# A second buffer for one decay tile, and two steps of the scan placed behind the projection in a Mamba-2 layer

## The chip, the cores and the metric

The kernel runs on one core of one Trainium2 chip. The metric is device time in microseconds, as the median of several runs. The engines are PE (TensorE: matmuls, with PEld for its weight loads), DVE (VectorE), ACT (ScalarE), POOL (GpSimd) and SP (SyncE), whose queue issues the DMAs. Each engine takes its instructions in the order of its own queue.

## The reference

Two layers run over a context pass of 128 tokens and a denoising pass of 512 tokens, with shared weights and width 1024. Layer 0 is gated attention; the change doesn't touch it. Layer 1 is a bidirectional Mamba-2 scan in chunks of 128 tokens, so there are five tiles of tokens: tile 0 is the context, tiles 1 to 4 are the denoising pass. What matters here, for each of four groups of eight heads:

```
proj = h @ w_in;  z, xbc, dt = split(proj)
xbc  = silu(depthwise_conv(xbc, width 3))          # x, B and C
cb     = C @ B^T                                    # per tile, 128 x 128
y_diag = (cb * decay) @ x                           # decay: exp of differences of cumulative sums, per head
states = B^T @ (x * decay_end)
h      = h * chunk_decay + states                   # from tile to tile
y_off  = (C @ h_prev) * exp(a_cs)
y = y_forward + flip(y_backward) + d_skip * x
out = rms_norm(y * silu(z)) @ w_out
```

Both directions have a decay tile of their own. The kernel adds the two before it multiplies by C.B, so one diagonal product per tile serves both.

## The kernel before, in words

Matrix products of activations and weights are done as three products of high and low parts. `split` makes a high part (a cast on ScalarE, L73) and a low part (a difference on VectorE or GpSimd, L74). Weights come through `raw` tiles (two buffers) and become `wh` and `wl` tiles.

Layer 1 works through four groups `g` of heads. In each there are ten steps `j`. Steps 1 to 5 deal with one tile each in the order `seq = [0, 2, 3, 1, 4]`. In a step the source lists, in this order:

- `mix` (L1127, L1128): the product C.B of the tile of the step before on PE, into a slot of the PSUM pool `a` (four slots), then the decay tile `am0` is multiplied by it on VectorE.
- `off` (L1173 to L1175) and `advance` (L1179, L1182, L1183) for both directions: the product of C and the state, scaled and added to `Y`, and the new state.
- `decay` (L1116, L1117, L1121, L1122): two affine selects on GpSimd, sixteen exponentials on ScalarE, and GpSimd's sum of the two directions' tiles `am0` and `am1`.
- `diag` (L1135, L1138 to L1140): sixteen products of the decay tile with x into a PSUM slot, four transposes of `Y` into another, a copy on ScalarE and a sum on VectorE. After `diag` the `am0` buffer is free.
- `a_load` (L1112): the loads of the next tile's `am0` (two buffers) and `am1` (one buffer), 512 KB each, on SP's queue.
- the fill: the projection of a chunk of the next group's x, B or C (`proj_T`, L914: 48 matmuls into one of two `pj` tiles of PSUM), its convolution on VectorE (L994 to L996, tanh L998 on ScalarE, L999), the transposes of the chunk before (L1007), or a chunk of z (L1057, L1058). In the last group the fill holds z, the turn of finished tiles (L1354, L1357) and the first matmuls of the output weights (L1368).

`gate` and `gate_last` (L1086, L1094 to L1098) multiply `Y` by the gate and add up its squares. `final_rstd` (L1373, L1374) sums the squares over partitions.

The kernel is built with `schedule_with_timeline_sim=True`: a planner plays the program through with costs of its own and sets the order on each engine from that. The order in the source is a priority, and no more; an instruction that isn't ready in the planner's account is overtaken. `high_priority(offset=300)` moves the priority of what it encloses ahead by 300; `issue_after(i)` puts what it encloses, on the engine of instruction `i`, behind `i`.

## Time and profile before

| what | value |
|---|---|
| runs | 994.69, 998.58 and 999.16 us, median 998.58 |
| profiled execution | 996.55 us, of which the span is 994.8 |
| PE busy | 937.9 us, 94% |
| DVE, ACT, POOL busy | 656.3 (66%), 515.3 (52%), 431.1 us (43%) |
| mean granted clock of PE over the span | 0.981 of full speed |

Busy time is the time in which an engine has an instruction in work. Matmuls overlap, so a matmul's own duration is longer than its distance to the next. The granted clock is 1.00 (2.4 GHz) or 0.50 (1.2 GHz) at any moment. In a row of the order in time, the bracket at the end is the time that the engine stood idle before it, and what it waited for. "A <- B: 7.5, 2, 5.2" in a list of waits says that A waited for B 7.5 us in total, twice, and 5.2 us at the longest.

### The profile page before, as it was taken

The page shows a single profiled execution, that of the slowest core. Times are in us where ns is not written, and L with a number is a line of the kernel's source. Part 1 is how long each engine was busy: PE and PEld are TensorE (multiplying, and loading weights), DVE is VectorE, ACT ScalarE, POOL GpSimd, SP SyncE. Part 2 cuts the span into 40 slices and gives each one's busy share as a digit, 9 for nine tenths or more (in the row PEclk, how much of TensorE's full clock was granted, in tenths as well). Part 3 has the DMA queues.
Part 4 walks back from the last instruction along what each step waited for, and adds up shares of the span by engine and source line. Part 5 has one row for each costly group of instructions (what it writes and reads, how often), then busy time and mean ns, then how long its engine had stood idle before and what let it go on. Part 6 is the DMA issues. An engine that isn't in the chain of part 4 may idle for free. (4 is left out here: it accounts for less than half of the span.)

```text
span 994.8 us, 17000 instructions
## 1 busy us (share of the span) xinstructions
PE 937.9 (94%) x6466; PEld 835.0 (84%) x6466; DVE 656.3 (66%) x1046; ACT 515.3 (52%) x1212; POOL 431.1 (43%) x415
## 2 busy tenths in 40 slices
PE   5998999999999989989899979999999999989998
PEld 3897879879997789989898878889988898658786
DVE  5468665666675764884759854956587547797663
ACT  5355666757775763433446564446436642554240
POOL 3345235227270162364267475739484853333000
PEclk9999999999999989999999999999999999989999
DMA  9942234221113222333234352344524441455752
GB/s 319 351 128 87 86 127 138 67 73 43 37 49 107 85 93 100 123 106 89 86 131 148 121 181 88 109 139 145 151 87 146 156 133 64 128 183 190 257 194 96
DMA packets 90354, 127.91 MB, mean 129 GB/s; under 512 B 6816, under 2 KB 65312, under 8 KB 90272
## 3 DMA queue, kind: packets, MB, share of 16 engines
q1 hardware_dynamic: 90272, 126.82, 39.6%
q8 instruction: 51, 0.84, 0.3%
q14 instruction: 31, 0.25, 0.1%
HBM read 115.10 MB, written 11.70 MB: 127 GB/s over the span
## 5 line engine op out<-in xcount | busy, mean ns | idle before, releaser
L914 PE MATMUL pj<-h,wh 128*128 128x322 f32 (+1 forms) x1248 | 298.3, 325 | 8.7 <-DVE B L999 7.5
L914 PEld LDWEIGHTS pj<-h,wh 128*128 128x128 f32 (+1 forms) x1248 | 211.2, 189 | 21.5 <-issue 14.0
L74 POOL TENSOR_TENSOR wl<-raw,wh 128x512 fp32r<-128x512 f32 (+1 forms) x70 | 133.1, 1912 | 184.6 <-ACT wh L73 182.9
L914 PE MATMUL pj<-h,wl 128*128 128x322 f32 (+1 forms) x624 | 198.6, 319 | 0.0
L73 ACT CAST wh<-raw 128x1024 fp32r<-128x1024 f32 (+1 forms) x117 | 103.0, 912 | 79.7 <-DMA raw<-in_l_w_out 22.4
L1121 ACT ACTIVATE am<-am,nb 128x128 f32<-128x128 f32 x320 | 97.9, 389 | 62.4 <-POOL am L1117 39.9
L914 PEld LDWEIGHTS pj<-h,wl 128*128 128x128 f32 (+1 forms) x624 | 118.2, 190 | 3.9 <-issue 3.6
L283 PE MATMUL pp<-wh,big 128*128 128x256 f32 x576 | 112.1, 284 | 0.5 <-ACT sg L527 0.5
L283 PEld LDWEIGHTS pp<-wh,big 128*128 128x128 f32 x576 | 91.2, 188 | 0.9 <-ACT sg L527 0.7
L74 DVE TENSOR_TENSOR wl<-raw,wh 128x1024 fp32r<-128x1024 f32 x47 | 62.8, 1347 | 38.0 <-ACT wh L73 38.0
L283 PE MATMUL pp<-wl,big 128*128 128x256 f32 x288 | 81.1, 282 | 0.0
L74 DVE TENSOR_TENSOR pl<-pt,ph 128x512 fp32r<-128x512 f32 (+1 forms) x100 | 59.2, 599 | 25.9 <-ACT ph L73 25.1
L633 DVE TENSOR_REDUCE nm<-S 128x1 f32<-128x640 f32 x64 | 52.3, 819 | 13.7 <-PE S L630 12.7
L73 ACT CAST ph<-pt 128x512 fp32r<-128x512 f32 (+1 forms) x100 | 51.4, 517 | 19.1 <-PE pt L658 14.3
L1122 POOL TENSOR_TENSOR am<-am,am 128x1024 f32<-128x1024 f32 x20 | 48.7, 2437 | 26.2 <-ACT am L1121 26.2
L637 ACT ACTIVATE Pt<-S,nm 128x640 f32<-128x640 f32 x64 | 51.2, 802 | 13.4 <-PE pt L658 9.9
L1368 PE MATMUL pj<-wh,h 128*128 128x512 f32 x160 | 54.4, 413 | 0.5 <-ACT wh L73 0.5
L283 PEld LDWEIGHTS pp<-wl,big 128*128 128x128 f32 x288 | 54.3, 188 | 0.0
L658 PE MATMUL pt<-cst,Pt 128*128 128x128 f32 x320 | 51.6, 279 | 2.6 <-DVE pl L74 2.3
L630 PE MATMUL S<-kT,qT 128*128 128x320 f32 x256 | 51.1, 324 | 2.3 <-ACT Pt L637 2.3
L1116 POOL TENSOR_SCALAR_AFFINE_SELECT am<-am 128x1024 f32<-128x1024 f32 x20 | 24.2, 1211 | 56.6 <-DMA am<-acd 32.3
L658 PEld LDWEIGHTS pt<-cst,Pt 128*128 128x128 f32 x320 | 37.2, 142 | 11.8 <-PE S L630 3.7
(347 smaller groups left out, 2135.9 us busy)
## 6 DMA issues: line engine op xcount, KB each, us to landing
raw<-in_l_w_in SPq DMA_DIRECT2D x48, 512.0 KB
am<-acd SPq DMA_DIRECT2D x40, 512.0 KB
raw<-in_l_w_out SPq DMA_DIRECT2D x36, 512.0 KB
og<-in_l_mod_w SPq DMA_DIRECT2D x29, 512.0 KB
raw<-in_l_w_in SPq DMA_DIRECT2D x25, 256.0 KB
mw<-in_l_mod_w SPq DMA_DIRECT2D x11, 512.0 KB
raw<-in_l_mod_w SPq DMA_DIRECT2D x8, 512.0 KB
yzd<-ys SPq DMA_DIRECT2D x6, 640.0 KB
```

The costliest lines, as they stand in the source:

```text
L73: (heng.tensor_copy if heng else self.nc.scalar.copy)(hi, src)
L74: (eng or self.nc.vector).tensor_tensor(lo, src, r32(hi), op=ALU.subtract)
L283: nc.tensor.matmul(ps, a[:, k, cs], b[:, k, :], start=k == 0 and a is hi and b is w[0], stop=k == KD - 1 and a is lo)
L630: nc.tensor.matmul(S[:, 192 + 320 * q:512 + 320 * q], qTs[g, t][:, h, :], kT[:, hl, 320 * q:320 * q + 320], start=hl == 0, stop=hl == 1)
L633: nc.vector.tensor_reduce(c["m"], c["s"], axis=AX.X, op=ALU.max, negate=True)
L637: nc.scalar.activation(Pt, c["s"], AF.Exp, bias=c["m"], scale=1.0, accum_out=rss[g][t][:, h:h + 1])
L658: nc.tensor.transpose(pt[:, 2 * i + j, :], Pts[j][:, kt * P:kt * P + P], self.ident)
L914: nc.tensor.matmul(ps[0:m, 190 + 322 * half:512 + 322 * half], w[b][:, k, off:off + m], hT[s][:, k, 322 * half:322 * half + 322], start=fi ...
L1116: nc.gpsimd.affine_select(out=af[0], in_=af[0], pattern=[[0, 8], [1, P]], base=0, channel_multiplier=-1, compare_op=ALU.is_ge, fill=NEG)
L1121: nc.scalar.activation(af[d][:, h, :], af[d][:, h, :], AF.Exp, bias=self.nb[:, t, i:i + 1], scale=1.0)
L1122: nc.gpsimd.tensor_tensor(af[0], af[0], af[1], op=ALU.add)
L1368: nc.tensor.matmul(self.PS[t][n], y[a][:, kk, :], b, start=k0 + k == 0 and i == 0, stop=k0 + k == 15 and i == 2)
```

## The change

The second direction's decay tile `am1` gets two buffers (in every place that uses the tag). The five instructions of a convolution get a priority ahead by 300. `mix` and `diag` move behind the fill of their step, and `mix` on VectorE is tied behind the last VectorE instruction that was listed before it. In the last group `final_rstd` comes two steps later than `gate_last`.

```
--- before.py
+++ after.py
@@ -68,6 +68,9 @@
         kw = {} if space is None else {"space": space}
         p = self.tc.tile_pool(name=name, bufs=bufs, side=side, reuse_waits="tile", **kw) if space != DRAM else self.tc.tile_pool(name=name, bufs=bufs, space=DRAM)
         return ctx.enter_context(p)
+
+    def last_on(self, engine):
+        return next(i for i in reversed(self.nc.cur_bb.bb.instructions) if i.engine == engine)
 
     def split(self, hi, lo, src, eng=None, heng=None):
         (heng.tensor_copy if heng else self.nc.scalar.copy)(hi, src)
@@ -922,7 +925,7 @@
         nc.sync.dma_start(out=misc[:, 200:], in_=A["cst"][:, 3 * P + 2:])
         upper, lower = misc[:, 200:200 + P], misc[:, 200 + P:]
         ones, al, db = misc[:, 0:P], misc[:, P:P + 64], misc[0:64, 199:200]
-        packs = [self.tl(wk, [P, 3, NT, 64], tag=t_, bufs=b_) for t_, b_ in (("am0", 2), ("am0", 2), ("am1", 1))]
+        packs = [self.tl(wk, [P, 3, NT, 64], tag=t_, bufs=b_) for t_, b_ in (("am0", 2), ("am0", 2), ("am1", 2))]
         slots = iter([p_[:, i] for p_ in packs for i in range(3)])
         self.dsk = self.tl(sp, [P, SH], tag="dsk")
         for d, s in enumerate(("f", "b")):
@@ -991,12 +994,13 @@
         ps = self.proj_T(pj, w, off, P, hT)
         cb0 = self.col["l1_conv_b"][0]
         n = TW - 3
-        nc.vector.tensor_scalar(out=u, in0=ps[:, 1:1 + n], scalar1=self.cw[:, 24 + j:25 + j], scalar2=self.cols[:, cb0 + j:cb0 + j + 1], op0=ALU.mult, op1=ALU.add)
-        nc.vector.scalar_tensor_tensor(out=u, in0=ps[:, 0:n], scalar=self.cw[:, j:j + 1], in1=u, op0=ALU.mult, op1=ALU.add)
-        nc.vector.scalar_tensor_tensor(out=u, in0=ps[:, 2:2 + n], scalar=self.cw[:, 48 + j:49 + j], in1=u, op0=ALU.mult, op1=ALU.add)
         th = ps[:, 1:1 + n]
-        nc.scalar.activation(th, u, AF.Tanh)
-        nc.vector.scalar_tensor_tensor(out=u, in0=th, scalar=1.0, in1=u, op0=ALU.add, op1=ALU.mult)
+        with self.tc.high_priority(offset=300):
+            nc.vector.tensor_scalar(out=u, in0=th, scalar1=self.cw[:, 24 + j:25 + j], scalar2=self.cols[:, cb0 + j:cb0 + j + 1], op0=ALU.mult, op1=ALU.add)
+            nc.vector.scalar_tensor_tensor(out=u, in0=ps[:, 0:n], scalar=self.cw[:, j:j + 1], in1=u, op0=ALU.mult, op1=ALU.add)
+            nc.vector.scalar_tensor_tensor(out=u, in0=ps[:, 2:2 + n], scalar=self.cw[:, 48 + j:49 + j], in1=u, op0=ALU.mult, op1=ALU.add)
+            nc.scalar.activation(th, u, AF.Tanh)
+            nc.vector.scalar_tensor_tensor(out=u, in0=th, scalar=1.0, in1=u, op0=ALU.add, op1=ALU.mult)
         return u
 
     def turn(self, u, pa, put):
@@ -1107,7 +1111,7 @@
             nc.gpsimd.tensor_tensor(h3(y), h3(xts[g][:, t, :]), bch(self.dsk[:, 8 * g:8 * g + 8]), op=ALU.mult)
 
         def a_load(g, t):
-            af = W[g, t] = [self.tl(wk, [P, 8, P], tag=f"am{d}", bufs=2 - d) for d in range(2)]
+            af = W[g, t] = [self.tl(wk, [P, 8, P], tag=f"am{d}", bufs=2) for d in range(2)]
             for d in range(2):
                 nc.sync.dma_start(out=af[d].rearrange("p h l -> p (h l)"), in_=self.acd[t][g][d].rearrange("h l -> (h l)").unsqueeze(0).to_broadcast([P, 8 * P]))
 
@@ -1238,8 +1242,6 @@
                 fl = {j: [nx(j)] for j in range(4)}
                 fl.update({4: ([zf(0)] if g else []) + [lambda: x_turn(g + 1, 3)], 5: [zf(1)] if g else [], 6: [lambda: bc_unit(g + 1, 0)], 7: [lambda: bc_unit(g + 1, 1)], 8: [zf(2), lambda: b_turn(g + 1)], 9: [zf(3)]})
             for j in range(10):
-                if 1 <= j <= 5:
-                    mix(g, seq[j - 1])
                 if 1 <= j <= 4:
                     for d in range(2):
                         off(g, j if d == 0 else 5 - j, d)
@@ -1256,8 +1258,6 @@
                         y_init(g, t)
                 if j < 5:
                     decay(g, seq[j])
-                for t in {1: (0,), 3: (2, 3), 4: (1,), 5: (4,)}.get(j, ()):
-                    diag(g, t)
                 if j < 4:
                     a_load(g, seq[j + 1])
                 if j <= 2:
@@ -1268,10 +1268,16 @@
                         weighted(g, 0, d)
                 for f in fl.get(j, []):
                     f()
+                if 1 <= j <= 5:
+                    with tc.issue_after(self.last_on(mybir.EngineType.DVE)):
+                        mix(g, seq[j - 1])
+                for t in {1: (0,), 3: (2, 3), 4: (1,), 5: (4,)}.get(j, ()):
+                    diag(g, t)
                 if last:
+                    for t in {6: (2, 3), 7: (1, 0), 8: (4,)}.get(j, ()):
+                        self.final_rstd(t, pa)
                     for t in {4: (2, 3), 5: (1, 0), 6: (4,)}.get(j, ()):
                         gate_last(t)
-                        self.final_rstd(t, pa)
                     continue
                 if j == 6:
                     gate(g, 0)
@@ -1292,7 +1298,7 @@
         hold2(2, 3, wk, "Wh", 1)
         hold2(3, 3, wk, "Wl", 1)
         rest = (1, 4, 0)
-        hold2(0, 0, wk, "am1", 1)
+        hold2(0, 0, wk, "am1", 2)
         for t in rest[:2]:
             hold2(t, 0, wk, "am0", 2)
         self.gate_alloc(1, sp, wk, "xs", "xt", 2)
@@ -1328,7 +1334,7 @@
         w = [self.load_wide(wp, A["l1_w_out"], k0) for k0 in (12, 14)]
         xr = {}
         for t, tag in zip(rest, ("am0", "am0", "am1")):
-            xr[t] = self.tl(wk, [P, D], tag=tag, bufs=2 - int(tag[2]))
+            xr[t] = self.tl(wk, [P, D], tag=tag, bufs=2)
             nc.sync.dma_start(out=xr[t], in_=self.x1d[t])
         for t in rest:
             if t:
```

## Rows read from the trace of the kernel before

**Rows 1.** Group stages: length; busy PE, PEld, DVE, ACT, POOL; clock; DMA share; GB/s

```profile
513.00:605.00 92.00, 86.45 (x578) 77.02 (x576) 65.64 (x76) 56.52 (x154) 58.91 (x39) 0.98 0.42 129
605.00:698.00 93.00, 90.31 (x608) 80.68 (x607) 60.80 (x73) 49.37 (x123) 60.47 (x42) 1.00 0.44 133
698.00:797.00 99.00, 95.13 (x646) 86.16 (x645) 66.97 (x79) 51.66 (x129) 62.14 (x44) 1.00 0.42 134
797.00:895.00 98.00, 91.06 (x513) 75.53 (x511) 68.74 (x83) 43.33 (x93) 38.34 (x30) 0.95 0.39 125
```

**Rows 2.** The chain that ended last: start, us, and what ran

```profile
794.90 7.39 PE pj L914 x48
```

**Rows 3.** PE's waits from 513 to 895 us: total, times, longest

```profile
PE pj L914 <- DVE B L999: 7.5, 2, 5.2
PE a L1138 <- DVE ys L1175: 3.6, 4, 1.8
PE a L1135 <- DVE ys L1175: 2.3, 1, 2.3
...
PE a L1179 <- DVE am L1128: 1.2, 1, 1.2
PE a L1373 <- POOL ssq L1098: 1.1, 1, 1.1
```

**Rows 4.** Order in time on PE, around the stall at 589: start, us

```profile
581.92 0.31 PE L914 MATMUL pj<-h,wl 128*128 128x322 f32 x1
...
589.03 0.91 PE L914 MATMUL pj<-h,wh 128*128 128x322 f32 x2 [5.19 <-DVE B L999]
...
592.35 0.45 PE L914 MATMUL pj<-h,wh 128*128 128x322 f32 x2
```

**Rows 5.** Order in time on VectorE, ahead of that stall

```profile
579.71 1.22 DVE L1128 TENSOR_TENSOR am<-am,a 128x1024 f32<-128x1024 f32 x1 [1.39 <-POOL am L1122]
580.84 0.94 DVE L994 TENSOR_SCALAR B<-pj,cw,cols 128x641 f32<-128x641 f32 x1
...
588.17 0.81 DVE L999 SCALAR_TENSOR_TENSOR B<-pj,B 128x641 f32<-128x641 f32 x1
```

**Rows 6.** Order in time on SP's queue, then on GpSimd

```profile
569.71 0.34 SPq L1112 DMA_DIRECT2D am<-acd  x1
...
573.55 1.09 POOL L1117 TENSOR_SCALAR_AFFINE_SELECT am<-am 128x1024 f32<-128x1024 f32 x1 [3.87 <-DMA am<-acd]
577.28 2.39 POOL L1122 TENSOR_TENSOR am<-am,am 128x1024 f32<-128x1024 f32 x1 [2.63 <-ACT am L1121]
```

**Rows 7.** Waits of SP's queue over the whole span

```profile
SPq L1112 <- POOL am L1122: 68.3, 18, 10.5
SPq L1112 <- PE a L1135: 62.7, 15, 13.2
```

**Rows 8.** Order in time on ScalarE, ahead of the stall at 795

```profile
787.81 4.78 ACT L1121 ACTIVATE am<-am,nb 128x128 f32<-128x128 f32 x16
```

**Rows 9.** Order in time on PE, the first diagonal block

```profile
532.82 1.09 PE L1135 MATMUL a<-am,xt 128*64 128x128 f32 x16
```

**Rows 10.** Order in time: weight loads on SP's queue, their casts on ScalarE

```profile
563.79 3.95 SPq L83 DMA_DIRECT2D raw<-in_l_w_in  x2
...
583.58 1.98 ACT L73 CAST wh<-raw 128x1024 fp32r<-128x1024 f32 x2
```

**Rows 11.** PE in the last group: order in time, and the chain

```profile
854.96 1.90 PE L1135 MATMUL a<-am,xt 128*64 128x128 f32 x16 [2.26 <-DVE ys L1175]
...
887.32 7.80 PE pj L1368 x22
...
952.62 3.73 PE pj L1368 x16
```

**Rows 12.** Order in time on PE, in the softplus stage

```profile
478.24 0.76 PE L1007 MATMUL a<-cst,u 128*128 128x128 f32 x5 [2.34 <-DVE u L999]
```

**Rows 13.** Busy time in a stretch of 20 us, columns as in Rows 1

```profile
880.00:900.00 20.00, 16.09 (x73) 12.39 (x68) 18.49 (x23) 10.21 (x15) 8.06 (x10) 0.83 0.49 154
```

More of the change, by code (lines that the diff above doesn't have):

```diff
@@ L70, in pool, with last_on @@
         return ctx.enter_context(p)
+    def last_on(self, engine):
+        return next(i for i in reversed(self.nc.cur_bb.bb.instructions) if i.engine == engine)
     def split(self, hi, lo, src, eng=None, heng=None):
@@ L924, in dt_stage @@
         ones, al, db = misc[:, 0:P], misc[:, P:P + 64], misc[0:64, 199:200]
-        packs = [self.tl(wk, [P, 3, NT, 64], tag=t_, bufs=b_) for t_, b_ in (("am0", 2), ("am0", 2), ("am1", 1))]
+        packs = [self.tl(wk, [P, 3, NT, 64], tag=t_, bufs=b_) for t_, b_ in (("am0", 2), ("am0", 2), ("am1", 2))]
         slots = iter([p_[:, i] for p_ in packs for i in range(3)])
@@ L993, in conv_chunk @@
         n = TW - 3
-        nc.vector.tensor_scalar(out=u, in0=ps[:, 1:1 + n], scalar1=self.cw[:, 24 + j:25 + j], scalar2=self.cols[:, cb0 + j:cb0 + j + 1], op0=ALU.mult, op1=ALU.add)
-        nc.vector.scalar_tensor_tensor(out=u, in0=ps[:, 0:n], scalar=self.cw[:, j:j + 1], in1=u, op0=ALU.mult, op1=ALU.add)
-        nc.vector.scalar_tensor_tensor(out=u, in0=ps[:, 2:2 + n], scalar=self.cw[:, 48 + j:49 + j], in1=u, op0=ALU.mult, op1=ALU.add)
         th = ps[:, 1:1 + n]
-        nc.scalar.activation(th, u, AF.Tanh)
-        nc.vector.scalar_tensor_tensor(out=u, in0=th, scalar=1.0, in1=u, op0=ALU.add, op1=ALU.mult)
+        with self.tc.high_priority(offset=300):
+            nc.vector.tensor_scalar(out=u, in0=th, scalar1=self.cw[:, 24 + j:25 + j], scalar2=self.cols[:, cb0 + j:cb0 + j + 1], op0=ALU.mult, op1=ALU.add)
+            nc.vector.scalar_tensor_tensor(out=u, in0=ps[:, 0:n], scalar=self.cw[:, j:j + 1], in1=u, op0=ALU.mult, op1=ALU.add)
+            nc.vector.scalar_tensor_tensor(out=u, in0=ps[:, 2:2 + n], scalar=self.cw[:, 48 + j:49 + j], in1=u, op0=ALU.mult, op1=ALU.add)
+            nc.scalar.activation(th, u, AF.Tanh)
+            nc.vector.scalar_tensor_tensor(out=u, in0=th, scalar=1.0, in1=u, op0=ALU.add, op1=ALU.mult)
         return u
@@ L1109, in a_load @@
         def a_load(g, t):
-            af = W[g, t] = [self.tl(wk, [P, 8, P], tag=f"am{d}", bufs=2 - d) for d in range(2)]
+            af = W[g, t] = [self.tl(wk, [P, 8, P], tag=f"am{d}", bufs=2) for d in range(2)]
             for d in range(2):
@@ L1240, in layer1 @@
             for j in range(10):
-                if 1 <= j <= 5:
-                    mix(g, seq[j - 1])
                 if 1 <= j <= 4:
@@ L1258, in layer1 @@
                     decay(g, seq[j])
-                for t in {1: (0,), 3: (2, 3), 4: (1,), 5: (4,)}.get(j, ()):
-                    diag(g, t)
                 if j < 4:
@@ L1270, in layer1 @@
                     f()
+                if 1 <= j <= 5:
+                    with tc.issue_after(self.last_on(mybir.EngineType.DVE)):
+                        mix(g, seq[j - 1])
+                for t in {1: (0,), 3: (2, 3), 4: (1,), 5: (4,)}.get(j, ()):
+                    diag(g, t)
                 if last:
+                    for t in {6: (2, 3), 7: (1, 0), 8: (4,)}.get(j, ()):
+                        self.final_rstd(t, pa)
                     for t in {4: (2, 3), 5: (1, 0), 6: (4,)}.get(j, ()):
                         gate_last(t)
-                        self.final_rstd(t, pa)
                     continue
@@ L1294, in layer1 @@
         rest = (1, 4, 0)
-        hold2(0, 0, wk, "am1", 1)
+        hold2(0, 0, wk, "am1", 2)
         for t in rest[:2]:
@@ L1330, in layer1 @@
         for t, tag in zip(rest, ("am0", "am0", "am1")):
-            xr[t] = self.tl(wk, [P, D], tag=tag, bufs=2 - int(tag[2]))
+            xr[t] = self.tl(wk, [P, D], tag=tag, bufs=2)
             nc.sync.dma_start(out=xr[t], in_=self.x1d[t])
```

## The prediction

> **What bounds the kernel now.** I read busy time by stage first, then who makes the tensor engine (PE) wait, then the order of the other engines around each such wait. PE is by far the busiest engine in all four group stages of the second layer [rows 1]. A projection runs without holes: 48 matmuls in 7.39 us, 0.154 us each [rows 2]. So the time can fall only by what PE stands idle and by what it loses at the lower clock behind an idle stretch. In the four stages (513 to 895 us) PE idles 5.55, 2.69, 3.87 and 6.94 us, 19.1 together [rows 1]. Five lines of waits carry most of it [rows 3], of three kinds: a projection that finds both its PSUM tiles (`pj`) unread because a convolution is late on VectorE (7.5 us in two waits); diagonal products, transposes and state products that stand in PE's queue and wait for `Y` or for a PSUM slot (3.6 + 2.3 + 1.2); and the sums of squares (1.1).
>
> **The largest stall, step by step.** PE does nothing for 5.19 us before 589.03 [rows 4]. It waits for the last convolution instruction on B, which starts at 588.17 [rows 5]. That convolution's first instruction started only at 580.84. PE ended the second of the two B/C projections by 582.2 [rows 4]; the first was ready one projection (7.4) and perhaps 1.7 us of small products earlier, near 573 (an estimate from these rows). VectorE could have begun then, but the product by C.B (L1128, 1.22 us) stood ahead of it in VectorE's queue at 579.71, and waited for GpSimd's sum of the two decay tiles [rows 5]. The sum (L1122, at 577.28) waited for ScalarE's exponentials, those for the affine select at 573.55, and that for the second direction's tile, whose load was issued at 569.71, when its one buffer came free [rows 6]. SP's queue spends 68.3 us, in 18 waits, on that buffer (L1112 on L1122) and 62.7 us, in 15, on the first direction's two (L1112 on L1135) [rows 7].
>
> **The change, part by part.**
> *Second `am1` buffer.* It removes SP's 68.3 us, none of it PE's own. From the chain above it takes the load, 3.84 us from issue to select (569.71 to 573.55). It adds no instruction.
>
> *Convolution ahead of other work.* Four VectorE instructions of 0.81 to 0.94 us and a tanh of about that size make some 4.3 us (an estimate from [rows 5]); in the stall they took 8.1, from 580.84 to 588.98, with other work between. The second wait of this kind, 7.5 - 5.2 = 2.3 us [rows 3], ends at 794.90 [rows 2], behind a tanh that stood after sixteen exponentials of 4.78 us together [rows 8]. What now falls behind is the off and advance work, which frees PSUM slots; one slot that was late cost L1179 1.2 [rows 3]. Bound of the loss: nine steps (three in each of three groups) by 1.2, so 10.8 us; below, nothing, since PE has the next projection (7.4) in hand and that covers 4.3.
>
> *Product and diagonal products behind the step's work.* Twenty products of 1.22 us and the matmuls of twenty diagonal blocks remain as they are. In PE's queue the move is smaller than the source suggests: the first diagonal block already comes at 532.82, behind the projection that stands after it in the source [rows 9]. What changes is that PE no longer reaches the transposes just when `Y` is being summed. The move itself issues no DMA, but a diagonal block frees an `am0` buffer, so the loads of the fourth and fifth tile leave later, by up to a projection and a convolution (7.4 + 4.3 = 11.7). Behind them in SP's queue stand the weights: today two weight loads are issued from 563.79 to 567.74, and cast only at 583.58, when the weight buffer is free [rows 10]. That leaves 15.8 us, 12.0 after a transfer of 3.84, just above 11.7, so I put this at nothing. Without that cover it costs up to 11.7 - 7.4 = 4.3 us a group.
>
> *Final sums of squares two steps later.* This takes the 1.1 us of L1373 [rows 3] away; the weight matmuls between hide it.
>
> **The sum**, each term with its clock dip.
> 1. The stall at 589: 5.19, and the 12 matmuls from 589.03 to 592.35 took 3.32 instead of 12 x 0.154 = 1.85 [rows 4]. 6.7.
> 2. The stall at 795: 2.3.
> 3. Waits inside the steps: L1138 without its longest, 3.6 - 1.8, and 1.2 of L1179 [rows 3]. 3.0.
> 4. The wait at 854.96: 2.26, and its 16 products took 1.90 us where they take 1.09 [rows 9, 11]. 3.1.
> 5. From 882 to 895: 1.8 and 1.1 of waits [rows 3], and 22 matmuls in 7.80 us where 16 take 3.73 (0.233 each, so 5.1 for 22), 2.7 of clock [rows 11]. 5.6.
> 6. The 2.34 at 478.24, a transpose that waits for a convolution in the softplus stage [rows 12]. 2.3.
> All of it is 23.0. I take terms 1 to 4 whole, 15.1. Of term 5 half, 2.8, because VectorE there is busy 18.49 of 20 us [rows 13] and a wait taken from one instruction falls on the next weight split. Of term 6 1.0: the softplus chain keeps its place beside the convolution. That is 18.9. Against it stand new waits: every engine's order is planned anew, and even the group without a large stall idles 2.69 us [rows 1]; I take two such, 5.4. Net 13.5: 996.55 becomes 983.1. The profiled execution lies 2.0 under the median of the runs (998.58) and 1.9 over the fastest, so I add one: 984.
>
> **The rivals.**
> *Only the stalls by the convolution go*, the move being empty because PE's queue already has it. Then 6.7 + 2.3 are won, perhaps 1 more: 987. For it speaks the block at 532.82 [rows 9]; against it L1138's four waits for `Y` [rows 3].
> *Given back.* What is won in the middle only brings PE sooner to waits on VectorE, 92% busy from 880 to 900 [rows 13]. Term 1 stays, and new waits near 5 eat the rest: 995.
> *Slower, by the first direction's buffers.* A diagonal block comes 11.7 us later, and the next product is ready 3.84 + 1.09 + 2.39 + 2.39 = 9.7 us behind it (load, select, half of the sixteen exponentials, sum [rows 6, 8]), or 15.6 for a second tile behind the first (another 1.09 + 2.39 + 2.39). If that product stands in VectorE's queue ahead of the next convolution, PE has 7.4 us of projection and then stops for 2.3 to 8.2 us, some 5.3, and 1.5 of clock, in four groups: 27 against 18.9 won, so 1005. It decides once VectorE waits over 7.4 us at L1128; today the wait there is 1.39 in the worst stall [rows 5]. Against it: convolutions now go first, and the other direction's tile is there early.
> *Much faster.* The Trainium skill, "Perfetto Trace Analysis" (Identifying the Most-Contended Engine), holds that matmul busy time is a poor measure of what PE has left, and weight loading a good one. In the four stages weight loads fill 319.4 of 382 us, so 62.6 are empty against 19.1 by matmuls [rows 1]; were nine tenths of that to close, the time would be near 940. By that rule there is room that the sum does not count. The trace speaks against it: 0.154 us from one matmul to the next, 48 in a row, leaves no hole to close [rows 2].
>
> **How the numbers follow.** Forecast as summed, 973 to 993: 0.56. Only the convolution's stalls: 0.14. Much faster: 0.02. Given back: 0.15. Slower: 0.13. A difference of 0.5%, 5 us, is about what can be told from none in runs that spread from 994.69 to 999.16. So faster 0.72, same 0.15, slower 0.13. The range runs from everything won (996.55 - 23.0 = 973.5, a little below it for the clock) to no gain at 999, which leaves out the slower case and the much faster one.
>
> **What the profile after would show.** Right: no wait of PE above 3 us between 513 and 895, SP's wait of L1112 on L1122 nearly gone, the convolution's four instructions close together, PE idle in the four stages together under 10 us. Wrong: VectorE idle above 7 us before L1128, waits of PE on L999 that remain, loads of `am` that hold SP for 20 us with weight casts late behind them, or new PE waits on PSUM slots (L1173, L1179) of more than 1 us a step.

## The result, and the profile after

The changed kernel takes 1000.0 us (median of 20 runs, 997.41 to 1005.94), the kernel before beside it 995.25 (20 runs, 992.19 to 999.66). The ratio of the means is 1.0055, with a 95% interval of 1.004 to 1.0071: slower by about half a per cent. The prediction was 984, in a range from a little under 973.5 to 999, so both its direction and its range were wrong.

The profiled span grew by 3.2 us, from 994.8 to 998.0. PE's busy time did not change (937.9 us before, 938.0 after), so what the span gained is idle time of PE. To see where, I cut both spans at the first transpose of each group's initial states, the same instruction in both, and at the end of the projections (848.25 and 847.00). Columns as in [rows 1]. First the kernel before: the four groups (the fourth up to the end of the projections), and the stretch behind them.

```profile
513.85:605.46 91.61, 86.06 (x574) 76.63 (x573) 65.30 (x76) 56.98 (x155) 58.06 (x39) 0.98 0.43 129
605.46:700.22 94.76, 92.06 (x621) 82.44 (x619) 61.63 (x74) 50.17 (x125) 62.69 (x43) 1.00 0.43 131
700.22:809.85 109.63, 105.76 (x717) 96.78 (x716) 69.14 (x82) 55.52 (x140) 67.12 (x47) 1.00 0.42 132
809.85:848.25 38.40, 38.40 (x243) 34.20 (x241) 25.27 (x30) 11.44 (x21) 16.58 (x14) 1.00 0.27 90
848.25:895.00 46.75, 39.81 (x186) 28.50 (x184) 40.46 (x48) 26.77 (x58) 14.55 (x12) 0.89 0.51 160
```

Then the changed kernel.

```profile
512.76:613.35 100.59, 88.83 (x573) 79.39 (x572) 64.33 (x76) 62.77 (x171) 62.94 (x42) 0.95 0.40 125
613.35:704.31 90.96, 90.96 (x621) 82.38 (x619) 61.86 (x74) 45.24 (x108) 57.47 (x39) 1.00 0.41 125
704.31:802.70 98.39, 98.09 (x669) 89.48 (x668) 65.82 (x78) 53.23 (x135) 62.62 (x45) 1.00 0.45 140
802.70:847.00 44.30, 43.89 (x285) 40.45 (x284) 25.23 (x28) 13.97 (x27) 19.79 (x16) 1.00 0.33 104
847.00:900.00 53.00, 47.15 (x222) 33.58 (x222) 48.92 (x56) 28.37 (x59) 18.05 (x11) 0.94 0.48 158
900.00:930.00 30.00, 27.73 (x134) 21.03 (x133) 24.00 (x33) 13.16 (x16) 9.56 (x18) 1.00 0.60 203
930.00:998.00 68.00, 61.92 (x267) 49.51 (x265) 36.28 (x46) 17.39 (x21) 1.59 (x1) 0.99 0.48 163
```

PE's idle time is the length of a stretch less PE's busy time in it. In the second and third groups and up to the end of the projections the idle time falls from 2.70 + 3.87 + 0 to 0.00 + 0.30 + 0.41: 5.9 us gained. In the first group it rises from 5.55 to 11.76, and PE is busy 2.8 us longer with one matmul fewer, because its mean granted clock is 0.95 instead of 0.98: behind a hole it runs at the lower of its two levels, 1.2 GHz, for a while (the sixteen products at 590.09 below take 1.88 us, where the sixteen of [rows 9] take 1.09). That is 9.0 us lost in one group. After the projections the rest of the kernel takes 4.5 us more (998.0 - 847.0 against 994.8 - 848.25). Ahead of the first group, 1.1 us is gained (513.85 to 512.76). That is chance: 1.2 us of difference stand already at the first matmul of the second layer (432.52 and 431.32), ahead of everything that the change touches. So -1.1 + 9.0 - 3.8 - 5.3 + 4.5 make up the 3.2 us of the span (3.3 by these rounded terms), where -3.8 and -5.3 are the lengths of the second group and of the third and fourth together. Of the 5.3 some 2.2 are not idle time but work of PE that now comes behind the projections (105.76 + 38.40 busy before, 98.09 + 43.89 after).

PE's order in time in the changed kernel shows the large holes of the first and of the last group, with the idle time and what ended it. They answer to [rows 3, 4, 11].

```profile
535.05 0.84 PE L1011 MATMUL a<-cst,u 128*128 128x128 f32 x5 [3.50 <-DVE u L1003]
...
590.09 1.88 PE L1139 MATMUL a<-am,xt 128*64 128x128 f32 x16 [3.44 <-issue]
...
596.86 0.76 PE L917 MATMUL pj<-h,wh 128*128 128x322 f32 x2 [3.84 <-DVE B L1003]
...
857.35 0.79 PE L1374 MATMUL pj<-wh,h 128*128 128x512 f32 x1 [2.79 <-DVE xt L1062]
```

(Lines of the changed kernel stand 3 to 6 further down: L914 is L917, L999 is L1003, L1121 is L1125, L1135 is L1139, L1139 is L1143.) The stall of 5.19 us at 589 [rows 4] has become two of 3.44 and 3.84, and a new one of 3.50 stands at 535. In place of the wait of 2.26 at 854.96 [rows 11] stands another, of 2.79. In the runs below the lines shift again by a few; the operation and the tiles tell which one is meant. What [rows 7] showed has not become less either (waits of SP's queue over the whole span: total, times, longest):

```profile
SPq L1116 <- POOL am L1126: 88.2, 16, 10.5
SPq L1116 <- PE a L1139: 49.6, 15, 8.1
```

SP waited 68.3 us for the one `am1` buffer and now waits 88.2 for the two. This wait is no measure of the time: it is 66.8 us in e1 below, which is slower than the kernel before, and 101.3 in e15, one of the fastest.

**Who makes the new holes.** ScalarE's order ahead of the stall at 535, and then ahead of the one at 596.86 ("x32" is 32 instructions in a row):

```profile
516.91 9.46 ACT L1125 ACTIVATE am<-am,nb 128x128 f32<-128x128 f32 x32
526.27 1.98 ACT L76 CAST wh<-raw 128x1024 fp32r<-128x1024 f32 x2
528.16 0.70 ACT L1002 ACTIVATE pj<-u 128x641 f32<-128x641 f32 x1
...
589.53 2.45 ACT L1125 ACTIVATE am<-am,nb 128x128 f32<-128x128 f32 x8 [2.48 <-POOL am L1121]
592.90 2.45 ACT L1125 ACTIVATE am<-am,nb 128x128 f32<-128x128 f32 x8 [0.92 <-POOL am L1121]
595.25 0.69 ACT L1002 ACTIVATE pj<-B 128x641 f32<-128x641 f32 x1
```

With two tiles loaded ahead, the exponentials of two tiles stand together: 32 in a row, 9.46 us, ahead of two weight casts and of a tanh that the path needs. In the kernel before a cast came between the first eight and the next sixteen, and the tanh of the same convolution started at 526.90, not 528.16:

```profile
518.00 2.44 ACT L1121 ACTIVATE am<-am,nb 128x128 f32<-128x128 f32 x8
520.34 1.03 ACT L73 CAST wh<-raw 128x1024 fp32r<-128x1024 f32 x1
521.27 4.78 ACT L1121 ACTIVATE am<-am,nb 128x128 f32<-128x128 f32 x16
525.96 1.03 ACT L73 CAST wh<-raw 128x1024 fp32r<-128x1024 f32 x1
526.90 0.70 ACT L998 ACTIVATE pj<-u 128x641 f32<-128x641 f32 x1
```

In the changed kernel near 596 the tanh of B stands behind sixteen exponentials, which waited 2.48 and 0.92 us for their selects. VectorE had finished its part of that convolution by 593.2 (L1001 started at 591.50, two of them in 1.66 us), and the tanh started at 595.25. Its last instruction then ran at 595.97 and PE went on at 596.86.

VectorE's order at the stall at 535 shows the second part of it, first in the changed kernel, then in the kernel before:

```profile
527.06 3.90 DVE L1186 TENSOR_TENSOR h<-h,cd 128x512 f32<-128x512 f32 x2
530.88 3.38 DVE L77 TENSOR_TENSOR wl<-raw,wh 128x1024 fp32r<-128x1024 f32 x1
534.18 0.81 DVE L1003 SCALAR_TENSOR_TENSOR u<-pj,u 128x641 f32<-128x641 f32 x1
```

```profile
528.80 0.69 DVE L1182 TENSOR_TENSOR h<-h,cd 128x512 f32<-128x512 f32 x1
529.40 1.22 DVE L74 TENSOR_TENSOR wl<-raw,wh 128x1024 fp32r<-128x1024 f32 x1
530.54 0.82 DVE L999 SCALAR_TENSOR_TENSOR u<-pj,u 128x641 f32<-128x641 f32 x1
531.27 0.68 DVE L1183 TENSOR_TENSOR h<-a,h 128x512 f32<-128x512 f32 x1
531.99 1.39 DVE L1182 TENSOR_TENSOR h<-h,cd 128x512 f32<-128x512 f32 x1
```

The tanh ended at 528.9, but the convolution's last step stood behind two state scalings and a weight split and started at 534.18. In the kernel before it started at 530.54, 3.64 us sooner, close to the size of the new hole (3.50). So it was not the tanh that this step waited for in the end: the tanh was 1.26 us later than before, but had ended 5.3 us ahead of the step. That the scalings and the split themselves ran slowly is taken up at the end.

The hole of 3.44 at 590.09, for which the view names nothing ("issue"), ends 0.1 us after VectorE's product by C.B, which the diagonal products read:

```profile
587.07 1.79 DVE L999 TENSOR_SCALAR B<-pj,cw,cols 128x641 f32<-128x641 f32 x2
588.78 1.20 DVE L1132 TENSOR_TENSOR am<-am,a 128x1024 f32<-128x1024 f32 x1
```

GpSimd's sum for it was done at 584.47 and PE's product C.B at 586.65, but on VectorE it stood behind the first steps of two convolutions. So what PE waits for here is the product in its new place.

### The profile page after: what moved, and what is told of

It is laid out like the page before. It is cut to its first block, busy times and chain, and to the rows that moved or that the text cites. A ratio compares the mean times of both kernels' runs of the same rounds, so it can differ in the third digit from the quotient of the medians.

```text
span 998.0 us, 17004 instructions
## 1 busy us (share of the span) xinstructions
PE 938.0 (94%) x6466; PEld 834.4 (84%) x6466; DVE 657.9 (66%) x1046; ACT 516.4 (52%) x1212; POOL 435.3 (44%) x415
## 5 line engine op out<-in xcount | busy, mean ns | idle before, releaser
L917 PE MATMUL pj<-h,wh 128*128 128x322 f32 (+1 forms) x1248 | 294.7, 322 | 5.5 <-DVE B L1003 4.2
L917 PEld LDWEIGHTS pj<-h,wh 128*128 128x128 f32 (+1 forms) x1248 | 212.5, 190 | 14.8 <-issue 7.8
L917 PE MATMUL pj<-h,wl 128*128 128x322 f32 (+1 forms) x624 | 199.5, 320 | 0.0
L1125 ACT ACTIVATE am<-am,nb 128x128 f32<-128x128 f32 x320 | 98.1, 389 | 52.6 <-POOL am L1121 27.7
L917 PEld LDWEIGHTS pj<-h,wl 128*128 128x128 f32 (+1 forms) x624 | 118.8, 190 | 3.9 <-issue 3.6
L77 DVE TENSOR_TENSOR wl<-raw,wh 128x1024 fp32r<-128x1024 f32 x47 | 69.4, 1483 | 28.8 <-ACT wh L76 28.8
```

The lines of the kernel that those rows point to most:

```text
L77: (eng or self.nc.vector).tensor_tensor(lo, src, r32(hi), op=ALU.subtract)
L917: nc.tensor.matmul(ps[0:m, 190 + 322 * half:512 + 322 * half], w[b][:, k, off:off + m], hT[s][:, k, 322 * half:322 * half + 322], start=fi ...
L1125: nc.scalar.activation(af[d][:, h, :], af[d][:, h, :], AF.Exp, bias=self.nb[:, t, i:i + 1], scale=1.0)
```

## The experiments

Four theories run through the experiments. A: the second buffer costs the time, because it lets later tiles' exponentials ahead. B: the move of the two products costs it. C: what costs is the order on ScalarE, exponentials ahead of the tanh and the copies that PE waits for. D: steps 4 and 5 of the first group hold no projection of their own, so PE has nothing to cover a late convolution there. (The "rival D" in the expectations of e5 to e7 is another one: stalls from VectorE's queue, or from GpSimd's work beside VectorE.) Each kernel was timed beside the kernel before on the same chip, in five rounds.

All of them in one table first. "First", "second on" and "rest" are lengths in us of the profiled execution: the first group; from there to the last matmul of the projections; from there to the last output matmul (L1368). Each length is of one execution. The first matmul of the second layer, ahead of which no edit reaches, comes between 430.97 and 434.65 us in the twenty of them, so one or two us in a single column may be chance.

| kernel | ratio to before, 95% interval | first | second on | rest |
|---|---|---|---|---|
| before | 1 | 91.6 | 242.6 | 141.7 |
| the change | 1.0055 [1.004, 1.0071] | 100.6 | 233.4 | 146.2 |
| e1 buffer alone | 1.0043 [1.0025, 1.0062] | 93.7 | 243.2 | 144.7 |
| e2 move alone | 1.0039 [1.0017, 1.0061] | 94.9 | 243.4 | 144.3 |
| e3 priority alone | 0.998 [0.9961, 0.9999] | 93.4 | 240.7 | 140.1 |
| e4 change without buffer | 1.0064 [1.004, 1.0087] | 95.4 | 240.1 | 147.4 |
| e5 change, exponentials tied | 0.9939 [0.9918, 0.9961] | 95.2 | 232.4 | 143.2 |
| e6 change, some tied | 1.0025 [1.0006, 1.0044] | 99.4 | 233.2 | 146.5 |
| e7 buffer, exponentials tied | 0.9925 [0.99, 0.995] | 94.4 | 234.6 | 141.1 |
| e8 change, last group as before | 1.0005 [0.9989, 1.0021] | 100.8 | 235.7 | 141.1 |
| e9 exponentials tied alone | 0.9997 [0.9981, 1.0012] | 96.5 | 235.4 | 143.4 |
| e10 buffer, tied, priority | 0.9905 [0.9887, 0.9923] | 90.7 | 234.7 | 142.5 |
| e11 buffer, tied, gate early | 0.9849 [0.9827, 0.987] | 84.2 | 236.1 | 141.7 |
| e12 e5, last group as before | 0.9936 [0.9915, 0.9956] | 94.6 | 234.4 | 138.6 |
| e13 gate early alone | 0.9937 [0.992, 0.9953] | 85.3 | 244.2 | 141.4 |
| e14 change, gate early | 1.0042 [1.0028, 1.0055] | 99.0 | 234.3 | 146.1 |
| e15 buffer, tied, priority, gate early | 0.9836 [0.9814, 0.9858] | 84.2 | 236.1 | 140.0 |
| e16 change, tied, gate early | 0.9917 [0.99, 0.9934] | 92.4 | 232.4 | 142.6 |
| e17 e15 and the move, product not held | 0.9881 [0.986, 0.9903] | 83.9 | 238.7 | 141.9 |
| e18 e15 and the diagonal products moved | 0.9828 [0.9804, 0.9852] | 84.3 | 236.1 | 141.6 |

**e1, the second buffer alone.**

```
-... (("am0", 2), ("am0", 2), ("am1", 1))]
+... (("am0", 2), ("am0", 2), ("am1", 2))]
...
-af = W[g, t] = [self.tl(wk, [P, 8, P], tag=f"am{d}", bufs=2 - d) for d in range(2)]
+af = W[g, t] = [self.tl(wk, [P, 8, P], tag=f"am{d}", bufs=2) for d in range(2)]
```

> The second am1 buffer alone, nothing moved and no priority. Theory A (the buffer does the harm: two tiles' exponentials, 32 in one row of 9.46 us in the changed kernel, come in front of the first tanh, and GpSimd's selects and sums fall beside VectorE's sums): slower than the kernel before by 3 to 8 us, with PE waits above 2 us before 605. Theory B (the move does it): no slower, 0 to 7 us faster, the stall of 5.19 us before 589 smaller or gone.

Slower, 1.0043. The sum L1122 of the tile at the old stall was now done at 572.25 (569.88 and 2.36 us), not at 579.67 [rows 6]. The path didn't use it. ScalarE, VectorE and PE, in order of time:

```profile
575.75 2.45 ACT L1121 ACTIVATE am<-am,nb 128x128 f32<-128x128 f32 x8 [3.43 <-POOL am L1117]
578.11 0.56 ACT L1139 COPY ys<-a 128x512 f32<-128x512 f32 x1
```

```profile
578.70 0.69 DVE L1140 TENSOR_TENSOR ys<-ys,a 128x512 f32<-128x512 f32 x1 [5.46 <-ACT ys L1139]
579.83 1.22 DVE L1128 TENSOR_TENSOR am<-am,a 128x1024 f32<-128x1024 f32 x1 [0.45 <-PE a L1127]
```

```profile
590.77 0.90 PE L914 MATMUL pj<-h,wh 128*128 128x322 f32 x2 [6.16 <-DVE B L999]
```

The exponentials of the next group's tile stand where the old ones stood: ScalarE waits 3.43 us for their select, the copy of `Y` waits behind them, VectorE waits 5.46 for the copy, and the product L1128 runs at 579.83, where it ran at 579.71 [rows 5]. PE's stall is 6.16 us instead of 5.19. The buffer gave the late work a later copy of itself.

**e2, the move alone**, with the product held behind VectorE's last instruction as in the change:

```
+                if 1 <= j <= 5:
+                    with tc.issue_after(self.last_on(mybir.EngineType.DVE)):
+                        mix(g, seq[j - 1])
+                for t in {1: (0,), 3: (2, 3), 4: (1,), 5: (4,)}.get(j, ()):
+                    diag(g, t)
```

> Only the product and the diagonal blocks behind the fill, with one am1 buffer, no priority, the final sums of squares where they were. Theory A: the same or up to 6 us faster (the wins of the second and third group without the loss of the first). Theory B (the move does the harm, by late diagonal blocks in the first group and by work pushed behind 895 us in the last): 3 to 8 us slower, PE idle in the first group above 8 us.

1.0039. The stall near 590 is nearly twice that of the kernel before. PE's row, and VectorE's product by C.B ahead of it:

```profile
589.92 1.98 PE L1138 MATMUL a<-am,xt 128*64 128x128 f32 x16 [9.48 <-ACT pj L1001]
```

```profile
588.60 1.22 DVE L1131 TENSOR_TENSOR am<-am,a 128x1024 f32<-128x1024 f32 x1 [2.19 <-POOL am L1125]
```

The view names a tanh (L1001), but the diagonal products read this product, which ended 0.1 us before them. It had waited for GpSimd's sum: with one buffer the sum is late, and PE's queue holds no projection ahead of the diagonal products in these steps.

**e3, the convolution's `high_priority` alone.**

> Only the convolution's priority. Both theories: the same to 4 us faster (the two waits of PE on the convolution of B, 7.5 us together, smaller). If neither theory holds and the priority does the harm, by off and advance sums that come late, it is slower by 2 us or more.

0.998, at the edge of what can be told from nothing. The two waits that were to become smaller did not: the stall near 590 is 6.12 us, and 2.48 us remain at 793.28, where the tanh still stands behind sixteen exponentials of 4.78 us, as in [rows 8].

**e4, the whole change without the buffer.**

> The whole change without the second am1 buffer. Theory A: faster than the kernel before by 3 to 8 us, and the first group's PE idle falls from 11.8 us to 6 or less. Theory B: as slow as the whole change or slower, 0.4% or more over the kernel before.

1.0064, with a stall of 9.70 us near 590 that ends like the one of e2 (the product from 589.52, after 2.19 us for the sum). So A and B are each half true: buffer and move cost 0.4% each by themselves, and they don't add up (1.0055 together with priority). Of these five only the whole change gains much from the second group on (233.4 against 240 to 243); the buffer with the move, or with priority alone, was not run untied.

**e5, the whole change with the exponentials held in source order on ScalarE:**

```
+                es.enter_context(tc.issue_after(self.last_on(mybir.EngineType.Activation)))
                 for d in range(2):
                     for h in range(8):
                         ...
```

> The whole change, and every tile's exponentials tied behind the ScalarE instruction that the source lists before them, so that no tanh and no copy of Y waits behind exponentials of a later tile. Theory C (the stalls of the first group come from ScalarE's queue: exponentials that wait for a late select stand ahead of the tanh of a convolution and the copy of Y, which the planner did not foresee): PE idle from 513 to the start of the second group falls from 11.8 us to 5 or less, and the time by 4 us or more against the changed kernel, to the kernel before or under it. Rival D (the stalls come from VectorE's queue, the product by C.B ahead of the convolution, or from GpSimd's work beside VectorE's): the idle stays above 8 us and the time within 2 us of the changed kernel's.

0.9939: this one line turns 0.55% of loss into 0.6% of gain. The wait of 3.50 at 535 is gone, and so is the one of 2.79 at 857. The stall near 590 is not: PE waits 6.25 there, until 0.1 us after the product by C.B, which again stands behind convolutions on VectorE. So neither expectation came whole: the time fell by 1.2%, more than theory C asked for, but PE's idle time in the first group is still 8.50 us, above both its 5 and the 8 of the rival.

**e6, the same tie for the first two tiles of groups 2 to 4 only.**

> The whole change, with only the first two tiles' exponentials of the second to fourth group tied in this way. Theory C, if it is the next group's exponentials: the stall of 3.84 us before the convolution of B goes, those of 3.50 and 3.44 stay, and the time falls by 3 to 5 us. Rival D: no difference beyond 2 us.

1.0025. The 3.84 at 596.86 became 0.92, but 3.78 stands before it and 3.50 at 535. The cost comes from the tiles inside a group too, not only from the next group's.

**e7, the second buffer with tied exponentials, no move, no priority.**

> The second buffer alone with all exponentials tied. Theory C: against the buffer alone (0.43% over the kernel before) it wins 4 us or more, and the stall of 6.16 us at 590 falls below 3. Rival D: as the buffer alone.

0.9925. The gain was as theory C has it, and its detail was wrong: the stall near 590 did not fall under 3 us, it is the only one of over 0.8 us left up to the end of the projections, and it grew to 8.23. The gain is from the second group on (234.6 against 242.6). That stall needed an explanation of its own (D).

**e8, the whole change with the old order of work in the last group.**

> The whole change, but in the last group the product, the diagonal blocks and the final sums of squares stay where they were. If the late work after 895 us costs what PE idles there beyond the kernel before (2.3 and 1.2 us), this is 2 to 4 us faster than the changed kernel, with the idle of the first group unchanged at about 11.8; if the last group's loss is only shifted, within 1 us of the changed kernel.

1.0005. The rest takes 141.1 us instead of 146.2, but 2.3 us of that are only shifted (235.7 instead of 233.4 before it). 2.8 us remain by these lengths, 0.5% by the ratio: that is what the new order, the move with the later final sums, costs in the last group. The first group still takes 100.8.

**e9, the tie alone**, on the kernel before, with one buffer.

> The kernel before with one buffer and its old order of work, and only the exponentials held in source order on ScalarE. Theory C (the order on ScalarE is what the change moved, the buffer by itself is worth nothing): 0.993 to 0.997 of before, within 3 us of the same tie with the second buffer (990). Rival (the tie frees the path only because the second buffer lets the loads and the causal selects run a tile ahead): 0.999 to 1.006, with waits of over 2 us in the second and third groups.

0.9997. The rival had the time right and its reason half wrong: there are no waits of over 2 us in the second and third groups (235.4 from there on, almost e7's 234.6), but the first group's stall grew to 9.20:

```profile
594.02 0.90 PE L917 MATMUL pj<-h,wh 128*128 128x322 f32 x2 [9.20 <-DVE B L1002]
```

So the tie gives some 7 us in the later groups with one buffer already, and loses it in the first group (+4.9), the rest (+1.7) and ahead of the groups. The second buffer then adds about 0.7% (0.9925 against 0.9997): the part that costs 0.4% by itself is a gain once ScalarE's order is held.

**e10, e7 with priority.**

> Second buffer, exponentials tied, and the convolution's priority, without the move. Theory C (once the exponentials are tied the convolution is not late, so priority has nothing to give): within 3 us of the same kernel without priority (990). Rival (priority still takes the convolution ahead of the weight split on VectorE in the first group's stall near 590): 983 to 987, with that stall under 5 us instead of 8.23.

0.9905; the stall near 590 is 4.23 us instead of 8.23, as the rival said, and the median of 986.81 is at the top of its 983 to 987.

**e11, e7 with the first group's third gate projection (z) at step 5 instead of step 8**, and a third buffer for it:

```
-4: ([zf(0)] if g else []) + ..., 5: [zf(1)] if g else [], ..., 8: [zf(2), lambda: b_turn(g + 1)]
+4: ([zf(0)] if g else []) + ..., 5: [zf(1 if g else 2)], ..., 8: ([zf(2)] if g else []) + [lambda: b_turn(g + 1)]
```

> Second buffer and tied exponentials, and in the first group the third gate projection goes from step 8 to step 5, with a third buffer for the gate. Theory D (the stall near 590 stands in every kernel because steps 4 and 5 of the first group hold no projection, so that TensorE has only waiting work left): the stall falls from 8.23 to under 3 us, and the time to 983 to 988. Rival (the projection waits for the same two projection buffers in PSUM as the ones behind it): the stall stays over 5 us and the time within 3 us of 990.

0.9849, 981.19 us: D is right. The first three groups, in columns as above:

```profile
513.00:597.20 84.20, 84.06 (x573) 75.24 (x572) 64.86 (x76) 48.29 (x123) 56.45 (x39) 1.00 0.41 127
597.20:689.80 92.60, 91.20 (x621) 82.32 (x620) 66.56 (x75) 50.12 (x123) 61.16 (x41) 1.00 0.47 149
689.80:795.10 105.30, 105.30 (x717) 96.73 (x716) 69.06 (x82) 53.27 (x132) 64.58 (x45) 1.00 0.41 129
```

PE is idle 0.14, 1.40 and 0 us in them, and the clock is full. The only wait that the view of PE's waits lists from 513 to 843 us is this one:

```profile
PE a L1133 <- ACT ys L1145: 1.4, 1, 1.4
```

**e12, e5 with the old order in the last group.**

> The whole change with tied exponentials, but the last group in the old order of work (mix and diagonal products at the head of a step). Theory (the two costs found add: exponentials in the first and last group, and work pushed past the last group's end by the move): 987 to 990, against 991.75 with the new order in all groups. Rival (the last group's gain and loss come from the position of the load alone): 991 to 993.

990.02, at the upper edge of the 987 to 990 that were expected. The rest falls from 143.2 to 138.6, but the second stretch grows by 2.0, and the ratio (0.9936) can't be told from e5's.

**e13, the early gate projection alone**, on the kernel before.

> The kernel before (one buffer, old order, nothing tied), with only the third gate projection of the first group at step 5 and a third gate buffer. Theory D (the empty steps are a cost of their own in every kernel): the wait at 589 is under 2.5 us and the time 0.992 to 0.996 of before. Rival (the gain needs the second buffer and the tied exponentials, which let the rest of the step be ready): 0.998 to 1.004, with a wait of over 4 us between 580 and 605.

0.9937, with 85.3 us in the first group instead of 91.6: PE idles 0.77 us in it (85.30 - 84.53) where it idled 5.55, and no stall near 589 is left. The empty steps were a cost of their own in the kernel before.

**e14, the whole change with the early gate projection.**

> The whole change as given, with only the third gate projection of the first group at step 5 and a third gate buffer. Theory D (the change's loss lies in the first group's empty steps): the first group falls from 100.6 to under 94 us and the time to 0.994 to 0.999 of before. Rival (the loss comes from exponentials ahead of the hyperbolic tangent on ScalarE, wherever TensorE's work stands): the waits of 3.5 and 3.8 us near 535 and 597 stay, the first group stays over 97 us, and the time is 1.001 to 1.006.

1.0042, 99.0 us in the first group. The rival is right, and D does not explain the change's loss. The wait at 536 stays, and the two near 590 become one, of 6.87 instead of 3.44 + 3.84:

```profile
536.04 0.86 PE L1011 MATMUL a<-cst,u 128*128 128x128 f32 x5 [3.47 <-DVE u L1003]
...
602.49 0.90 PE L1011 MATMUL a<-cst,B 128*128 128x128 f32 x3 [6.87 <-DVE B L1003]
```

**e15 and e16**, with the exponentials tied and the gate projection early: without the move (e15, with priority), and the whole change (e16).

> Second buffer, tied exponentials, early gate projection (981.19 in the run before) and the convolution's priority. Theory (priority took 2 to 3 us where the wait near 590 was, and that wait is gone): within 2 us of the kernel without priority. Rival (priority helps the last group, as it took out 1.6 us there alone): 977 to 979.

> The whole change with tied exponentials and the early gate projection. Theory (move of the mix and the diagonal products is worth nothing or less once the rest is ready in time): 980 to 985, not under the same without the move. Rival (the move is a gain once the first group is mended): 974 to 979.

e15 is 0.9836, 981.74 us, not to be told from e11: priority has nothing left to give. e16 is 989.56, slower than was expected by either theory. The whole change is some 8 us behind e15, and the first group alone loses that much (92.4 against 84.2; after it -3.7 and +2.6). This wait remains there:

```profile
596.30 1.33 PE L1011 MATMUL a<-cst,B 128*128 128x128 f32 x5 [5.44 <-DVE B L1003]
```

**e17 and e18**: e15 with parts of the move. e17 has both products moved, without `issue_after` for the one by C.B; e18 only the diagonal products. Both keep the final sums of squares in their old place.

> Second buffer, priority, tied exponentials, early gate projection, and the move of both products, but the product by C.B isn't held behind VectorE's last instruction. If the tie on VectorE makes the move's cost: within 3 us of the kernel without the move (981 to 985). If the place of the two in the step makes it: 988 to 992, with a wait of over 4 us before the first group's end, as with the tie.

> As the kernel without the move, but the diagonal products alone go behind the step's projection; the product by C.B stays at the head of the step. If the diagonal products' later place in TensorE's queue makes the cost: 986 to 992. If the product's later place makes it: 980 to 984, like the kernel without the move.

e18 is 0.9828: the diagonal products' new place costs nothing. e17 is 0.9881 (987.39 us), a little under the range for "the place makes it", but its first group is down to 83.9 us, as without the move; its loss comes after it (2.6 and 1.9 us). Between e16 and e17 only the hold differs, and the place of the final sums, which is in the last group. So the first group's 8 us come from holding the product by C.B behind VectorE's last instruction, and its later place as such costs elsewhere. Over the whole kernel the hold is not the larger part: the later place takes the ratio from 0.9836 to 0.9881, the hold, with the later final sums, from there to 0.9917, since the held kernel gets 6.3 us back from the second group on (232.4 against 238.7). e17's runs lie between 984.43 and 987.79, its profiled one near the low end, so the two are only roughly sized.

## Why the prediction was wrong, step by step

**What bounds the kernel: right.** PE's holes and its clock decide. The differences read above are holes in one of three stretches, and the slower matmuls behind them, and with the holes of the first three groups closed (e11) 1.5% of the time is gone.

**The second `am1` buffer: the first of two steps that failed.** The prediction says that it "takes the load, 3.84 us from issue to select", off the chain, and it did: in e1 the sum was ready 7.4 us earlier. The step then took for granted that each link behind it would start as much sooner. But the links stood in ScalarE's one queue, whose order the planner made from its own times, and it filled the room with the next tile's exponentials, ahead of the copy and the tanh. I had read the tanh behind sixteen exponentials at 795 [rows 8] and counted it as a stall to be won. It was the pattern that the buffer would multiply. The tie shows it: with the exponentials held in source order and no other edit, the change goes from 1.0055 to 0.9939 (e5), and the buffer from 1.0043 to 0.9925 (e7), where the same tie with one buffer gives nothing (0.9997, e9). It doesn't show through which engine the early exponentials cost most. The tie also moves GpSimd's sums, so at 535, where VectorE's slow instructions stand ahead of the step, the two are not told apart.

**Term 1, the stall at 589, 6.7 us: wrong in sign.** The first group lost 9.0 us, so this term alone misses by 15.7, more than the whole forecast gain of 13.5. The stall was explained by one chain, and three things stood there: the late product, a late tanh or copy on ScalarE behind exponentials, and steps 4 and 5 without a projection, so that any late convolution shows. The third is worth 6.3 us by itself (91.6 to 85.3 in e13, where no link of the predicted chain was touched). The sentence that PE "has the next projection (7.4) in hand and that covers 4.3" does not hold in these two steps, which have no projection.

**Terms 2 and 3, the stall at 795 and the waits inside the steps: the size came, by luck.** 5.3 us was forecast, and 5.9 us of idle time went, nearly all there was in the second and third groups. But the means that were named for it don't do it: priority alone leaves 2.48 us of the stall (e3), the move alone has waits of 4.53, 1.15 and 3.12 us in these groups (e2), and holding the exponentials does almost the same with neither (e9). Why the whole change clears them is open.

**Terms 4 to 6: nothing came.** In place of the wait of 2.26 at 854.96 stands one of 2.79 at 857.35, for a gate step (L1062) that stands behind a weight split of 3.33 us on VectorE; the softplus stage has 3.17 us of idle time where it had 3.13; and after the projections 4.5 us were lost. In the last group the move puts work past its end (by the old order e8 gets back 5.1 us there, 2.3 of them only shifted). I had taken half of term 5 because VectorE was full [rows 13]. The whole of it should have been left out.

**The move: the second step that failed, since the queue named was the wrong one.** I priced it by SP's queue and the weight loads behind `am0`, and put it "at nothing". e18 shows that moving the diagonal products does cost nothing. But with the exponentials tied and the gate projection early, the whole move with the later final sums costs 7.8 us (989.56 against 981.74, e16 and e15): about half by the later place of the product by C.B (e17 against e15), the rest by its hold behind VectorE's last instruction (with the later final sums), and the hold alone costs some 8 us in the first group (e16 against e17). The prediction named neither as an added wait, and that is how the move loses without the buffer as well (e2, e4). Taken together, the ratio goes from 1.0055 (the change) to 0.9939 by the tie, to 0.9917 by the early gate projection, to 0.9881 without the hold and with the final sums in their old place, and to 0.9836 without the move.

**New waits, 5.4 us: mis-sized.** New or grown holes in the first group alone are 6.2 us of idle time and 2.8 of clock, beside the 6.7 that did not go.

Of the prediction's signs of being wrong, one came plainly: PE still waits for the convolution's last step, 3.50 and 3.84 us in the first group.

**The rivals.** The time of 1000.0 lies midway between "given back" (995) and "slower" (1005). "Given back" had it right that term 1 stays, but it was to end as a small gain, and most of the loss is in the first group, not where VectorE is full. "Slower, by the first direction's buffers" had the sign and not the mechanism: VectorE waits 4.4 us at L1132 for the sum from 513 to 895, in two waits of at most 2.2, where 7.4 in one was the point from which that rival decides. What was held against it, that "convolutions now go first", was the weak spot, since the tanh in the middle of each is ScalarE's. "Much faster" by the weight loads' share did not come either: in e11 PE is idle 0.14 of 84.20 us in the first group while weight loads fill 75.24, so the rest of that time is not there to be won.

What stays open: why the last stretch gains or loses 1 to 5 us with almost every edit (138.6 to 147.4 in the table), and which of its instructions the move delays.

## What to carry to other kernels

When a transfer is made early by one more buffer, ask what each in-order engine behind it will now start earlier, and whether that goes ahead of something on the path; here the fix is to hold the early work in its place (one line, worth 1.2% with the buffer and nothing on the kernel before), and only then is the buffer a gain. The same kind of hold on work that the path needs costs: ask what stands ahead of it on its engine. A wait of SP's queue for a buffer is no measure of what the buffer is worth: it is 66.8 us in the slower e1 and 101.3 in e15. And a stall that survives every edit of its supposed chain is worth a look at what PE could do instead: one projection, moved into an empty step, gave 6.3 us in that group by itself, and with the buffer and the tie it is in the fastest kernels here (981 to 982 us).

## What the runs showed of the hardware

Two kinds of element-wise instructions of VectorE with both inputs in SBUF took longer beside GpSimd. In the changed kernel two state scalings took 3.90 us, where one takes 0.69 at 528.80 in the kernel before, with GpSimd idle, and the weight split behind them 3.38, where it took 1.22 at 529.40, again with GpSimd idle. (The scaling at 531.99 in the kernel before ran beside a GpSimd product until 532.83, and took 1.39.) GpSimd's order in time in the same stretch:

```profile
526.51 2.41 POOL L1126 TENSOR_TENSOR am<-am,am 128x1024 f32<-128x1024 f32 x1 [0.31 <-ACT am L1125]
528.87 1.55 POOL L1121 TENSOR_SCALAR_AFFINE_SELECT am<-am 128x1024 f32<-128x1024 f32 x1
530.39 2.79 POOL L77 TENSOR_TENSOR wl<-raw,wh 128x1024 fp32r<-128x1024 f32 x1
533.13 2.08 POOL L1121 TENSOR_SCALAR_AFFINE_SELECT am<-am 128x1024 f32<-128x1024 f32 x1
```

GpSimd is busy without a break from 526.51 to 535.21, and its own select takes 1.55 and 2.08 us where it takes 1.09 alone [rows 6]. The convolution's last step, which reads PSUM and SBUF, took its usual 0.81 in the same stretch. The Trainium skill, "SBUF — State Buffer" (Who interferes with whom), says that a VectorE instruction with two SBUF inputs contends with a GpSimd instruction that reads SBUF, and one with at most one such input, outside its two-port modes, does not. These rows agree; no run here tried it by itself. In the twenty traces together, the 519 such splits with GpSimd idle take 1.21 to 1.23 us, and the 210 with GpSimd busy for nine tenths of their time or more take 1.21 to 3.41, so not every one of them is slowed. VectorE took 4.7 us longer for the three (3.90 + 3.38 - 2 x 0.69 - 1.22), right ahead of the hole of 3.50, so GpSimd's work at that time cost the path on VectorE too; that the second buffer brought it there is argued from the order, not shown by a run.
